# A hybrid decoder trunk on one NeuronCore: a gate block moved ahead of the first window scores, dense weights requested one pair earlier, merge splits written one product later

## The chip, the cores and the metric

The kernel runs on one core of a Trainium2 chip. The time is the device time of one execution in microseconds (us). Three runs of the kernel before gave 2102.69, 2104.17 and 2104.78 us; the median, 2104.17 us, is the time before.

## The reference

Two layers of a decoder trunk work on a sequence of 1024 positions with 1024 channels, in float32. Each layer normalises its input and multiplies it by one wide matrix, whose columns feed three token mixers and their gates:

```python
h = rms_norm(x, g_pre)
p = h @ w_in
(u_a, v_a, gate_a, q_b, k_b, v_b, gate_b,
 q_c, k_c, v_c, gate_c, merge_logits) = jnp.split(p, offsets, axis=-1)
y_a = chunk_gmlp(u_a, v_a, ...) * silu(gate_a)
y_b = sliding_window_attention(rope(q_b), rope(k_b), v_b, sinks) * silu(gate_b)
y_c = stick_breaking_attention(q_c, k_c, v_c) * silu(gate_c)
gates = sigmoid(merge_logits + b_merge)
merged = gates[0]*(y_a @ w_branch_a) + gates[1]*(y_b @ w_branch_b) + gates[2]*(y_c @ w_branch_c)
x = x + rms_norm(merged @ w_out, g_post)
```

Branch B has 8 query heads of 64 channels, rotary positions on queries and keys, a window of 128 positions and a learned sink per head. The merge logits are 3 x 1024 columns, more than a third of the columns of `w_in`.

## The kernel before

Every float32 operand is kept as two parts, a rounded high part and the rest. `split` (L104-112) makes them: ACT casts the high part (L111) and DVE subtracts it from the operand (L112). Every product is then three matmuls on PE, `mm3` (L126-130): high by high (L128), high by low (L129), low by high (L130). All work arrays of 1024 columns come from 27 slots of SBUF, handed out by `new()` and given back by `done()` in first-in, first-out order. Raw weights land in tiles `wr` (two buffers), their split parts live in a tag `w` with six buffers, and there are two PSUM buffers for each of three tags (`pj`; `z` with the tile `pz`; `ta` with the tiles `ptr` and `pav`).

The order of PE's instructions is the order in which the program writes them. The other engines, and SP, which issues the DMAs, get their order from the framework's scheduler, which goes by priorities and by when it reckons that an instruction can start; what it chose is fixed in the program, and each engine works its list off from the front.

A layer runs through these stages:

- A stream of projection jobs (`stream`, filled by `queue_layer`). One job projects 128 columns of `w_in` for all positions: 48 matmuls of 128x512. `raw` makes the jobs of branch B's raw queries, `gate` those of the gate paths. ACT empties the PSUM tile of a query job (L275), then `after_q` applies `rope`: four DMAs swap halves of the channels (L288, on SP), POOL multiplies by sine and cosine (L289, L290), DVE adds (L291), and ACT and DVE split the result into two tiles by heads (L342, L343). `need(x)` runs the stream on PE up to and including job x; `fill(n)` runs n units of it, a job being 10 to 11 units.
- Branch C, with jobs of the stream between its own steps.
- Branch B (`branch_b`): `scores(v)` for v = 0 to 7, two for each pair of heads `hp`; each is 16 matmuls (L486), then copies by ACT and DVE (L492-499), the row maximum (L503), 8 exponentials (L507) with the sum on ACT, and a product by the reciprocal on DVE (L511). `transp` turns the result through PE (L519), `split` makes its parts and POOL masks them (L526); `attend` multiplies by the values (L543). Between these, `fill(FB[..])` gives PE jobs of the stream. The start is `need(("qb", 0))`, `fill(5)`, `scores(0)`, `fill(FB[0])` with `FB[0]` = 10, `scores(1)`.
- The dense stage (`dense`): 13 pairs of column blocks of 256 (a last gate block and the merge logits), each done by Strassen's way in 7 products of 12 matmuls. `prep(p)` loads a pair's weights in two DMAs (L733-737), makes the seven operands (POOL at L748, L750, L751 and L758, `split` for each), one at a time through a generator that `prod` keeps five operands ahead. DVE combines the products (L795). For a merge block ACT applies the sigmoid with the bias (L818) and SP stores the result to DRAM as `sg` (L819). Gate tasks (L708-713: SP's loads and stores, DVE, ACT) are done along the way.
- The merges (`merges`): branches c, b, a in this order, 8 row blocks each, in two halves; per half 12 matmuls, a multiplication by the loaded gate on DVE (L909), an addition (L912; on POOL, on DVE for the last two row blocks of branch a), and for branch a a split of the sum (L111, L112).
- The output projection (`project_out`), which reads these parts, the residual and the norms.

Of the kernel before, what the change touches and what calls it, by code (L numbers as in the profile page):

```python
# [22 lines left out]
P = 128  # L23
T = 1024
D = 1024
KD = D // P
# [7 lines left out]
O_M = 4864  # L34
NSLOT = 27
FC = (1.2, 1.2, 1.9, 1.2)
FB = (10, 1.9, 1.9, 2.2, 2.8, 2.8)
FB_MORE = {1: 2.3, 2: 1.3}


# [1 line left out]
def trunk(ctx, tc, x, w_in, gm_w_s, gm_b_s, gm_g, sinks, w_ba, w_bb, w_bc, b_merge, w_out,  # L42
# [198 lines left out]
    def queue_layer(l, S):  # L241
# [116 lines left out]
        gate("b", 3)  # L358
        for hp in range(4):
            raw(("qb", hp), O_QB + hp * P, 0.125, lambda hp=hp: after_q(hp))  # L360
            if hp < 2:
                gate("a", hp)

        def ua(c):
            def ev(hf, acc):
# [105 lines left out]
    def branch_b(l, S):  # L471
# [86 lines left out]
                nc.sync.dma_start(S["ob"][hp * P:(hp + 1) * P, :], o)  # L558
                done(o)

        need(("qb", 0))
        fill(5)
        ready = {0: scores(0)}
        fill(FB[0])
# [151 lines left out]
    def dense(l, S):  # L716

        T = S["T"].T
        pairs = [(O_GA + 2 * P, "g", ("a", 2))]
        pairs += [(O_M + "abc".index(br) * D + dm * P, "m", (i, br, dm)) for i, br in enumerate("cba")  # L720
                  for dm in range(0, KD, 2)]

        def rhs(nm, k):
            if nm in T:
                hi, lo = T[nm][k // 2]
                return [t.rearrange("p (k t) -> p k t", k=2)[:, k % 2] for t in (hi, lo)]
            hf, kh = {"B11": (0, 0), "B21": (0, 1), "T3": (1, 0), "B22": (1, 1)}[nm]
            return h[hf][0][:, kh * 4 + k], h[hf][1][:, kh * 4 + k]

        def prep(p):  # L730

            col = pairs[p][0]
            raw = []  # L733
            for q in range(2):
                t = wp.tile([P, 4, 256], F32, name="wr", tag="wr", bufs=2)
                nc.sync.dma_start(t, w_in[l, q * 512:(q + 1) * 512, col:col + 256].rearrange("(k p) c -> p k c", p=P))
                raw.append(t)
            a11, a21, a12, a22 = (raw[q][:, :, r * P:(r + 1) * P] for q in range(2) for r in range(2))

            def op(r):  # L740
                w = wp.tile([P, 2, 4, P], F32R, name="wop", tag="w", bufs=6)
                split(w[:, 0], w[:, 1], r)
                return w
            yield op(a11)
            yield op(a12)
            t3 = new()
            s3 = t3[:, :512].rearrange("p (k c) -> p k c", k=4)
            nc.gpsimd.tensor_tensor(s3, a11, a21, op=ALU.subtract)  # L748

            nc.gpsimd.tensor_tensor(a21, a21, a22, op=ALU.add)  # L750
            nc.gpsimd.tensor_tensor(a11, a21, a11, op=ALU.subtract)  # L751
            yield op(a11)
            w = op(s3)
            done(t3)
            yield w
            yield op(a21)
            yield op(a22)
            nc.gpsimd.tensor_tensor(a12, a12, a11, op=ALU.subtract)  # L758
            yield op(a12)

        ops = []
        preps = [prep(p) for p in range(len(pairs))]

        def left(n):
            while len(ops) <= min(n, 7 * len(pairs) - 1):
                ops.append(next(preps[len(ops) // 7]))

        def prod(n, nm):
            left(n + 5)
            w, acc = ops[n], bank()  # L770
            for k in range(4):
                mm3(acc, (w[:, 0, k], w[:, 1, k]), rhs(nm, k), k == 0, k == 3)
            return acc

        left(3)
        S["T"].go(0)
        while step() is not None:
            pass
        S["T"].go(0)
        assert S["T"].left is None  # L780
        S["T"].place_t3()
        a = branch_a(l, S)
        next(a)
        tasks = deque([lambda br=br, c=c: gate_task(S, br, c) for br in "cba" for c in range(4)])
        then = {0: lambda: next(a), 1: lambda: (next(a), next(a)), 2: lambda: (next(a), next(a))}
        for p, (col, kind, what) in enumerate(pairs):
            n = 7 * p
            u = new()
            out = [new(), new()]
            u2, u3 = u[:, :512], u[:, 512:]  # L790
            c11, c12, c21, c22 = (t[:, j * 512:(j + 1) * 512] for t in out for j in range(2))

            def add(o, x, b):
                with tc.high_priority():
                    nc.vector.tensor_tensor(o, x, b, op=ALU.add)  # L795
            p1 = prod(n, "B11")
            if p == len(pairs) - 1:
                S["first"] = load_y(S, "c", True)
            with tc.high_priority():
                nc.scalar.copy(c12, p1)  # L800
            add(c11, c12, prod(n + 1, "B21"))
            add(u2, c12, prod(n + 2, "T2"))
            if p in then:
                then[p]()
            add(u3, u2, prod(n + 3, "T3"))
            p5 = prod(n + 4, "T1")
            add(c22, u3, p5)
            add(u2, u2, p5)
            add(c21, u3, prod(n + 5, "T4"))
            add(c12, u2, prod(n + 6, "B22"))  # L810
            done(u)
            for j in range(2):
                if kind == "g":
                    br, c = what
                    nc.sync.dma_start(S["g" + br][(c + j) * P:(c + j + 1) * P, :], out[j])
                else:
                    i, br, dm = what
                    nc.scalar.activation(out[j], out[j], AF.Sigmoid, bias=bmv(l, "abc".index(br), dm + j))  # L818
                    nc.sync.dma_start(S["sg"][(i * KD + dm + j) * P:(i * KD + dm + j + 1) * P, :], out[j])  # L819
            done(*out)  # L820
            if p >= 1 and tasks:
                tasks.popleft()()
                if p % 2 and tasks:
                    tasks.popleft()()
        assert not tasks
        for t in T.values():
            for q in t:
                done(*q)
# [34 lines left out]
    def merges(l, S):  # L863
# [4 lines left out]
        order = ["c", "b", "a"]  # L868
        blocks = [(bi, br, dm) for bi, br in enumerate(order) for dm in range(KD)]
        wl, sgs = {}, {}  # L870

        def load(i):
            if i < len(blocks) and i not in wl:
# [14 lines left out]
        for i, (bi, br, dm) in enumerate(blocks):  # L888
# [11 lines left out]
            for hf in range(2):  # L900
# [4 lines left out]
                with tc.high_priority():  # L905
                    if bi == 0:
                        nc.vector.tensor_tensor(acc[dm][:, ts], sg[:, ts], z, op=ALU.mult)
                    else:
                        nc.vector.tensor_tensor(sg[:, ts], sg[:, ts], z, op=ALU.mult)  # L909
                if bi:  # L910
                    eng = nc.vector if bi == 2 and dm > KD - 3 else nc.gpsimd
                    eng.tensor_tensor(acc[dm][:, ts], acc[dm][:, ts], sg[:, ts], op=ALU.add)  # L912
                if bi == 2:
                    split(hi[:, ts], lo[:, ts], acc[dm][:, ts])
            done(sg)
            if bi == 2:
                done(acc[dm])
                mg.append((hi, lo))
            if bi == 0 and dm < 4:
                ys.setdefault("b", []).extend(load_y(S, "b", c=dm))  # L920
# [5 lines left out]
                load_wo(l, 0, dm * 2)  # L926
            if bi == 1 and dm == KD - 1:
                done(*S["yslots"])
        return mg

    xs = [x] + [dr.tile([T, D], F32, name=f"xs{l}") for l in range(1, L)] + [out]
# [174 lines left out]
```

## Time and profile before

| | |
|---|---|
| median of 3 runs | 2104.17 us (2102.69 to 2104.78) |
| profiled execution, its time | 2100.85 us |
| its span, first to last instruction | 2099.1 us |
| PE busy | 2034.7 us, 97% |
| DVE busy | 1171.5 us, 56% |
| ACT busy | 780.6 us, 37% |
| POOL busy | 497.9 us, 24% |
| mean granted TensorE clock | 0.990 |
| DMA moved | 245.03 MB, mean 117 GB/s |

The times of the trace count from the start of the span, so 1.75 us of the profiled execution's 2100.85 us lie around it. Busy PE is not PE at its peak: at the half level of the clock a matmul takes longer and still counts as busy. Layer 1 repeats layer 0 some 1040 us later.

### The profile page before, as it was taken

The page shows a single profiled execution, that of the slowest core. Times are in us where ns is not written, and L with a number is a line of the kernel's source. Part 1 is how long each engine was busy: PE and PEld are TensorE (multiplying, and loading weights), DVE is VectorE, ACT ScalarE, POOL GpSimd, SP SyncE. Part 2 cuts the span into 40 slices and gives each one's busy share as a digit, 9 for nine tenths or more (in the row PEclk, how much of TensorE's full clock was granted, in tenths as well). Part 3 has the DMA queues.
Part 4 walks back from the last instruction along what each step waited for, and adds up shares of the span by engine and source line. Part 5 has one row for each costly group of instructions (what it writes and reads, how often), then busy time and mean ns, then how long its engine had stood idle before and what let it go on. Part 6 is the DMA issues. An engine that isn't in the chain of part 4 may idle for free. (4 is left out here: it accounts for less than half of the span.)

```text
span 2099.1 us, 26470 instructions
## 1 busy us (share of the span) xinstructions
PE 2034.7 (97%) x10289; PEld 1700.7 (81%) x10289; DVE 1171.5 (56%) x1521; ACT 780.6 (37%) x1437; POOL 497.9 (24%) x485
## 2 busy tenths in 40 slices
PE   8999998999999999999999999989999999999998
PEld 7898886799887788887898988867988877888876
DVE  5455543468667766544545555344786676565433
ACT  5334333445324334212334334244553343432121
POOL 0121211133542331240002112112344333202400
PEclk9999999999999999999999999999999999999999
DMA  4112122112168538633321111312112775466213
GB/s 161 41 51 67 55 91 70 61 51 71 40 223 285 175 132 290 229 101 91 109 72 50 42 61 60 102 60 71 61 46 76 255 256 171 159 252 220 81 51 130
DMA packets 156253, 245.03 MB, mean 117 GB/s; under 512 B 8104, under 2 KB 113632, under 8 KB 156128
## 3 DMA queue, kind: packets, MB, share of 16 engines
q1 hardware_dynamic: 156128, 243.34, 34.6%
q8 instruction: 81, 1.33, 0.3%
q14 instruction: 44, 0.36, 0.1%
HBM read 166.76 MB, written 71.30 MB: 113 GB/s over the span
## 5 line engine op out<-in xcount | busy, mean ns | idle before, releaser
L128 PE MATMUL pj<-h,whi 128*128 128x512 f32 x968 | 392.4, 405 | 0.0
L129 PE MATMUL pj<-h,whi 128*128 128x512 f32 x968 | 383.5, 396 | 0.0
L130 PE MATMUL pj<-h,wlo 128*128 128x512 f32 x968 | 382.8, 395 | 0.0
L130 PEld LDWEIGHTS pj<-h,wlo 128*128 128x128 f32 x968 | 182.3, 188 | 43.7
L128 PEld LDWEIGHTS pj<-h,whi 128*128 128x128 f32 x968 | 183.2, 189 | 36.0
L129 PEld LDWEIGHTS pj<-h,whi 128*128 128x128 f32 x968 | 183.0, 189 | 34.3
L112 DVE TENSOR_TENSOR wop<-wr,wop 128x512 fp32r<-128x512 f32 x156 | 144.2, 929 | 109.3 <-ACT wop L111 105.9
L112 DVE TENSOR_TENSOR wlo<-wr,whi 128x1024 fp32r<-128x1024 f32 x96 | 128.8, 1342 | 93.6 <-ACT whi L111 93.2
L111 ACT CAST whi<-wr 128x1024 fp32r<-128x1024 f32 x96 | 100.5, 1049 | 185.9 <-PE pj L129 99.4
L111 ACT CAST wop<-wr 128x512 fp32r<-128x512 f32 x156 | 96.1, 617 | 183.8 <-DMA wr<-in_w_in_dram 102.1
L128 PE MATMUL pj<-whi,h 128*128 128x256 f32 x512 | 146.9, 287 | 0.0
L130 PE MATMUL pj<-whi,h 128*128 128x256 f32 x512 | 143.7, 281 | 0.6 <-DVE h L112 0.6
L398 DVE TENSOR_TENSOR_SCAN s<-s,ones 128x128 f32<-128x128 f32 (+3 forms) x64 | 88.4, 1382 | 99.1 <-POOL s L393 98.9
L129 PE MATMUL pj<-wlo,h 128*128 128x256 f32 x512 | 143.5, 280 | 0.0
L112 DVE TENSOR_TENSOR s<-ptr,s 128x512 fp32r<-128x512 f32 (+2 forms) x132 | 77.6, 592 | 106.6 <-ACT s L111 106.1
L912 POOL TENSOR_TENSOR s<-s,s 128x512 f32<-128x512 f32 x56 | 77.5, 1387 | 235.2 <-DVE s L909 130.2
L111 ACT CAST s<-ptr 128x512 fp32r<-128x512 f32 (+2 forms) x132 | 66.8, 506 | 118.8 <-PE ptr L415 110.3
L128 PE MATMUL pj<-h,s 128*128 128x512 f32 x256 | 102.6, 401 | 4.9 <-ACT s L111 3.5
L393 POOL TENSOR_SCALAR_AFFINE_SELECT s<-s 128x128 f32<-128x128 f32 x64 | 23.3, 364 | 346.1 <-ACT s L392 339.7
L111 ACT CAST s<-s 128x512 fp32r<-128x512 f32 (+2 forms) x64 | 47.9, 751 | 150.8 <-POOL s L912 69.7
L130 PE MATMUL pj<-h,s 128*128 128x512 f32 x256 | 101.8, 398 | 1.8 <-DVE s L112 1.8
L129 PE MATMUL pj<-h,s 128*128 128x512 f32 x256 | 101.5, 396 | 0.0
(227 smaller groups left out, 4700.6 us busy)
## 6 DMA issues: line engine op xcount, KB each, us to landing
wr<-in_w_in_dram SPq DMA_DIRECT2D x124, 512.0 KB, 4.1
sg<-s SPq DMA_DIRECT2D x48, 512.0 KB, 5.0
s<-sg SPq DMA_DIRECT2D x48, 512.0 KB, 5.1
s<-in_x_dram SPq DMA_DIRECT2D x16, 512.0 KB, 4.3
wor<-in_w_out_dram SPq DMA_DIRECT2D x16, 512.0 KB, 3.7
s<-s SPq DMA_DIRECT2D x40, 128.0 KB, 2.3
gc<-s SPq DMA_DIRECT2D x8, 512.0 KB, 2.7
oc<-s SPq DMA_DIRECT2D x8, 512.0 KB, 2.8
```

Of the source, the lines that this page charges most:

```text
L111: nc.scalar.copy(hi, raw)
L112: nc.vector.tensor_tensor(lo, raw, hi.bitcast(F32), op=ALU.subtract)
L128: nc.tensor.matmul(acc, lh, rh, start=first, stop=False)
L129: nc.tensor.matmul(acc, lh, rl, start=False, stop=False)
L130: nc.tensor.matmul(acc, ll, rh, start=False, stop=last)
L393: nc.gpsimd.affine_select(t1[:, dg], t1[:, dg], pattern=[[-1, P]], compare_op=ALU.is_gt, fill=1.0, base=0, channel_multiplier=1)
L398: nc.vector.tensor_tensor_scan(t1[:, :kl][:, ::-1], t1[:, :kl][:, ::-1], ones.to_broadcast([P, kl]), 1.0, op0=ALU.mult, op1=ALU.mult)
L912: eng.tensor_tensor(acc[dm][:, ts], acc[dm][:, ts], sg[:, ts], op=ALU.add)
```

## The change

Three things are done, for both layers.

First, the gate block `ga1` is queued behind `qb2` instead of behind `qb1`, branch B starts with `need("ga0")` instead of `need(("qb", 0))`, and `FB[0]` is 4 instead of 10. Secondly, a pair's weights are asked for by a new function `begin`, called for pair p + 1 at the head of pair p; odd pairs above 2 get two of the 27 slots in place of the two `wr` buffers, and the stores of `sg` are issued by ACT instead of SP. Thirdly, in the last branch of the merges the split of a half is put into a list and called behind the multiplication of the next half.

```diff
-FB = (10, 1.9, 1.9, 2.2, 2.8, 2.8)
+FB = (4, 1.9, 1.9, 2.2, 2.8, 2.8)
...
             raw(("qb", hp), O_QB + hp * P, 0.125, lambda hp=hp: after_q(hp))
-            if hp < 2:
-                gate("a", hp)
+            if hp in (0, 2):
+                gate("a", hp // 2)
...
-        need(("qb", 0))
+        need("ga0")
         fill(5)
...
-            col = pairs[p][0]
-            raw = []
-            for q in range(2):
-                t = wp.tile([P, 4, 256], F32, name="wr", tag="wr", bufs=2)
-                nc.sync.dma_start(t, w_in[l, q * 512:(q + 1) * 512, col:col + 256].rearrange("(k p) c -> p k c", p=P))
-                raw.append(t)
+            begin(p)
+            raw, slots = raws.pop(p)
...
             nc.gpsimd.tensor_tensor(a12, a12, a11, op=ALU.subtract)
-            yield op(a12)
-
+            w = op(a12)
+            done(*slots)
+            yield w
...
+        def begin(p):
+
+            if p < len(pairs) and p not in begun:
+                begun.add(p)
+                raws[p] = ([], [])
+                for q in range(2):
+                    if p % 2 and p > 2:
+                        t = new()
+                        raws[p][1].append(t)
+                        t = t.rearrange("p (k c) -> p k c", k=4)
+                    else:
+                        t = wp.tile([P, 4, 256], F32, name="wr", tag="wr", bufs=2)
+                    col = pairs[p][0]
+                    nc.sync.dma_start(t, w_in[l, q * 512:(q + 1) * 512, col:col + 256]
+                                      .rearrange("(k p) c -> p k c", p=P))
+                    raws[p][0].append(t)
...
             n = 7 * p
+            begin(p + 1)
             u = new()
...
-                    nc.sync.dma_start(S["sg"][(i * KD + dm + j) * P:(i * KD + dm + j + 1) * P, :], out[j])
+                    nc.scalar.dma_start(S["sg"][(i * KD + dm + j) * P:(i * KD + dm + j + 1) * P, :], out[j])
...
+                if late:
+                    late.pop()()
                 if bi:
                     eng = nc.vector if bi == 2 and dm > KD - 3 else nc.gpsimd
                     eng.tensor_tensor(acc[dm][:, ts], acc[dm][:, ts], sg[:, ts], op=ALU.add)
                 if bi == 2:
-                    split(hi[:, ts], lo[:, ts], acc[dm][:, ts])
+                    def parts(hi=hi, lo=lo, a=acc[dm], hf=hf, ts=ts):
+                        split(hi[:, ts], lo[:, ts], a[:, ts])
+                        if hf:
+                            done(a)
+                    late.append(parts)
...
+        late.pop()()
         return mg
```

On PE the change moves whole matmuls and changes none. Between the last matmul of `qb0` and the first of `scores(0)` there were 24 matmuls of 128x512 (the first half of `ga0`), and there are now 72 (`ga0` and the first half of `qb1`). Between `scores(0)` and `scores(1)` there were 48 and are now 21; behind `scores(1)` come 18 as before, then the first transposes (L519), and the rest of the sequence up to `scores(2)` has the same counts.

ACT's list from the first scores of layer 0 on, before (L275 with `s24_3234` is the emptying of `qb1`'s first half):

```order
L492 COPY s23_3135<-pz_3136 128x2x128
L493 COPY s23_3135<-pz_3136 128x2x128
L498 COPY s23_3135<-pz_3151 128x512
L507 ACT_TABLE_LOAD
L507 ACTIVATE s23_3135,ls_3163<-s23_3135,mx_3162 128x128 x8
L508 ACTIVATE es_3164<-es_3164 128x8
L111 CAST whi_3331<-wr_3329 128x1024
L275 ACTIVATE s24_3234<-pj_3209 128x512
```

And the same place now (L275 with `s23_3189` empties `qb1`, first half from `pj_3164`, second half from `pj_3191`):

```order
L275 ACTIVATE s23_3189<-pj_3164 128x512
L492 COPY s24_3195<-pz_3196 128x2x128
L493 COPY s24_3195<-pz_3196 128x2x128
L498 COPY s24_3195<-pz_3211 128x512
L507 ACT_TABLE_LOAD
L507 ACTIVATE s24_3195,ls_3223<-s24_3195,mx_3222 128x128 x2
L275 ACTIVATE s23_3189<-pj_3191 128x512
L507 ACTIVATE s24_3195,ls_3223<-s24_3195,mx_3222 128x128 x6
L508 ACTIVATE es_3224<-es_3224 128x8
```

The first half of `qb1` is now emptied ahead of the first softmax, and the emptying of its second half stands between the second and the third of the 8 exponentials.

POOL's list at the same place, before (L494 masks the first scores, L526 the transposed ones, L289 and L290 are the rotary products of `qb1`):

```order
L494 AFFINE_SELECT s23_3135<-s23_3135 128x2x128
L526 AFFINE_SELECT s12_3306<-s6_3305 128x512 x2
L526 AFFINE_SELECT s13_3351<-s19_3350 128x512 x2
L289 TENSOR_TENSOR s9_3315<-s9_3315,s17_2857 128x1024
L290 TENSOR_TENSOR s24_3234<-s24_3234,s15_2856 128x1024
```

And now:

```order
L494 AFFINE_SELECT s24_3195<-s24_3195 128x2x128
L526 AFFINE_SELECT s22_3349<-s21_3348 128x512 x2
L289 TENSOR_TENSOR s4_3262<-s4_3262,s17_2857 128x1024
L290 TENSOR_TENSOR s23_3189<-s23_3189,s15_2856 128x1024
L526 AFFINE_SELECT s18_3375<-s13_3374 128x512 x2
```

The rotary products moved ahead of the second pair of masks, and still stand behind the first pair.

DVE's list at the end of the last branch of layer 0, before (L909 multiplies a half, L912 adds it, L112 with slots is the split of that half, L112 with `wor` that of an output weight):

```order
L909 TENSOR_TENSOR s19_7680<-s19_7680,pj_7758 128x512
L912 TENSOR_TENSOR s9_7138<-s9_7138,s19_7680 128x512
L112 TENSOR_TENSOR s18_7757<-s9_7138,s16_7756 128x512
L909 TENSOR_TENSOR s19_7680<-s19_7680,ptr_7775 128x512
L912 TENSOR_TENSOR s9_7138<-s9_7138,s19_7680 128x512
L112 TENSOR_TENSOR s18_7757<-s9_7138,s16_7756 128x512
L909 TENSOR_TENSOR s22_7718<-s22_7718,pz_7794 128x512
L912 TENSOR_TENSOR s20_7175<-s20_7175,s22_7718 128x512
L112 TENSOR_TENSOR h11_75<-wor_7832,h10_74 128x1024
```

And now, where the same two lines are numbered L928 and L933:

```order
L928 TENSOR_TENSOR s12_7678<-s12_7678,pj_7756 128x512
L933 TENSOR_TENSOR s10_7138<-s10_7138,s12_7678 128x512
L112 TENSOR_TENSOR s3_7755<-s10_7138,s21_7754 128x512
L928 TENSOR_TENSOR s12_7678<-s12_7678,ptr_7773 128x512
L933 TENSOR_TENSOR s10_7138<-s10_7138,s12_7678 128x512
L112 TENSOR_TENSOR s3_7755<-s10_7138,s21_7754 128x512
L928 TENSOR_TENSOR s11_7716<-s11_7716,pz_7792 128x512
L933 TENSOR_TENSOR s26_7175<-s26_7175,s11_7716 128x512
L112 TENSOR_TENSOR h11_75<-wor_7832,h10_74 128x1024
```

Slots differ; the sequence of lines doesn't.

## Rows read from the trace of the kernel before

**Rows 1.** The page's first part: busy time of each engine, its share of the span, and the count of its instructions.

```profile
PE 2034.7 (97%) x10289; PEld 1700.7 (81%) x10289; DVE 1171.5 (56%) x1521; ACT 780.6 (37%) x1437; POOL 497.9 (24%) x485
```

**Rows 2.** The view of waits, for PE: what PE stood still for, us in total, times, longest.

```profile
PE pz L486 <- DVE s L343: 25.1, 8, 7.8
...
PE pz L130 <- DVE wop L112: 5.3, 5, 1.9
...
PE pj L128 <- ACT s L111: 3.5, 2, 1.7
...
PE pj L130 <- DVE s L112: 1.8, 2, 0.9
...
PE pj L128 <- DVE s L909: 1.4, 2, 0.7
PE pz L128 <- ACT wop L111: 1.3, 2, 1.2
```

**Rows 3.** The view by stretches, for four stretches around the first and the third scores of each layer and one in the dense stage of layer 1: length, busy time (and count) of PE, PEld, DVE, ACT and POOL, the granted clock, the DMA share, GB/s.

```profile
360.30:370.50 10.20, 6.32 (x22) 5.54 (x23) 5.33 (x6) 3.32 (x5) 0.41 (x1) 0.50 0.00 0
401.30:408.10 6.80, 5.64 (x20) 4.98 (x21) 3.04 (x5) 1.70 (x4) 0.41 (x1) 0.50 0.00 0
1401.40:1408.20 6.80, 4.06 (x17) 3.76 (x18) 2.88 (x3) 2.67 (x4) 0.41 (x1) 0.50 0.00 0
1438.90:1445.70 6.80, 4.34 (x17) 3.99 (x18) 2.88 (x3) 2.54 (x5) 0.41 (x1) 0.50 0.00 0
1749.50:1752.90 3.40, 3.40 (x10) 2.65 (x9) 3.40 (x6) 1.29 (x3) 0.97 (x1) 0.50 0.01 5
```

**Rows 4.** The timeline of PE around the first and the third scores of layer 0: start, duration, what, and in brackets PE's idle time before it.

```profile
355.54 0.40 PE L130 MATMUL pj<-h,wlo 128*128 128x512 f32 x1
...
363.72 0.80 PE L486 MATMUL pz<-s,s 128*128 128x256 f32 x2 [7.79 <-DVE s L343]
...
364.98 3.36 PE L486 MATMUL pz<-s,s 128*128 128x256 f32 x14 [0.46 <-DVE s L343]
...
402.00 0.80 PE L486 MATMUL pz<-s,s 128*128 128x256 f32 x2 [3.92 <-DVE s L343]
```

**Rows 5.** The timeline of ACT, SP, POOL and DVE ahead of the first scores of layer 0: the way of `qb0` from its last matmul to the operands of `scores(0)`.

```profile
350.39 0.59 ACT L275 ACTIVATE s<-pj 128x512 f32<-128x512 f32 x1
...
351.00 2.43 SPq L288 DMA_DIRECT2D s<-s  x4
...
355.44 2.35 POOL L289 TENSOR_TENSOR s<-s,s 128x1024 f32<-128x1024 f32 x1 [29.68 <-DMA s<-s]
...
360.11 1.23 DVE L291 TENSOR_TENSOR s<-s,s 128x1024 f32<-128x1024 f32 x1 [8.38 <-POOL s L290]
361.37 2.11 ACT L342 CAST s<-s 64x1024 fp32r<-64x1024 f32 x2 [5.52 <-DVE s L291]
362.45 2.47 DVE L343 TENSOR_TENSOR s<-s,s 64x1024 fp32r<-64x1024 f32 x2 [1.11 <-ACT s L342]
```

**Rows 6.** The timeline of ACT, DVE and POOL behind the first scores of layer 0: one exponential, the emptying of a gate block by DVE, the last step of the softmax, a copy of the second scores, two masks on POOL, and the low part of a stream weight.

```profile
372.61 0.40 ACT L507 ACTIVATE s<-s,mx 128x128 f32<-128x128 f32 x1
...
374.33 0.69 DVE L249 COPY s<-pj 128x512 f32<-128x512 f32 x1 [2.89 <-PE pj L130]
...
376.38 1.22 DVE L511 TENSOR_TENSOR s<-s,ls 128x1024 f32<-128x1024 f32 x1
...
382.20 0.73 DVE L499 COPY_PREDICATED s<-mprev,pz 128x512 f32<-128x512 int32 x1 [3.46 <-ACT s L498]
...
387.97 1.36 POOL L526 TENSOR_SCALAR_AFFINE_SELECT s<-s 128x512 fp32r<-128x512 f32 x2 [20.45 <-ACT s L111]
...
391.86 1.22 DVE L112 TENSOR_TENSOR wlo<-wr,whi 128x1024 fp32r<-128x1024 f32 x1
```

**Rows 7.** The view by stretches, PE alone, for the part of each layer's dense stage that holds all its waits for weights, and for a part that holds none: length, PE busy (and its count of matmuls, here all 128x512), granted clock, DMA share, GB/s.

```profile
645.00:715.00 70.00, 66.56 (x277) 1.00 0.64 222
1680.00:1756.00 76.00, 71.45 (x291) 0.98 0.66 228
800.00:870.00 70.00, 70.00 (x302) 1.00 0.67 236
```

**Rows 8.** The costliest groups of ACT between 620 and 905 us, the dense stage of layer 0 (us busy, mean ns of one, idle time before them by releaser).

```profile
L111 ACT CAST wop<-wr 128x512 fp32r<-128x512 f32 x58 | 35.7, 616 | 63.3 <-DMA wr<-in_w_in_dram 33.1 <-POOL wr L751 21.7 <-PE ptr L130 3.3
L818 ACT ACTIVATE s<-s,vec 128x1024 f32<-128x1024 f32 x22 | 25.3, 1149 | 20.8 <-DVE s L795 20.8
L711 ACT ACTIVATE s<-s 128x1024 f32<-128x1024 f32 x10 | 10.6, 1062 | 23.0 <-DVE s L710 19.3 <-DMA wr<-in_w_in_dram 3.6
```

**Rows 9.** The page's DMA issues, two of them: count, KB each, median us from issue to landing.

```profile
wr<-in_w_in_dram SPq DMA_DIRECT2D x124, 512.0 KB, 4.1
sg<-s SPq DMA_DIRECT2D x48, 512.0 KB, 5.0
```

**Rows 10.** The view by stretches, PE alone, for the end of the merges of both layers, all matmuls 128x512; columns as in rows 7.

```profile
958.00:973.00 15.00, 11.67 (x43) 0.89 0.22 67
1997.00:2012.00 15.00, 11.66 (x48) 1.00 0.18 60
```

**Rows 11.** The timeline of DVE for two successive multiplications in the last branch of layer 0, on the way to that end.

```profile
955.74 0.68 DVE L909 TENSOR_TENSOR s<-s,pz 128x512 f32<-128x512 f32 x1
...
959.14 0.68 DVE L909 TENSOR_TENSOR s<-s,pj 128x512 f32<-128x512 f32 x1
```

More of the change, by code (lines that the diff above doesn't have):

```diff
@@ L758, in prep @@
             nc.gpsimd.tensor_tensor(a12, a12, a11, op=ALU.subtract)
-            yield op(a12)
+            w = op(a12)
+            done(*slots)
+            yield w
+        raws = {}
+        def begin(p):
[13 more added lines that the diff above has]
+                    raws[p][0].append(t)
+        begun = set()
         ops = []
@@ L870, in merges @@
         wl, sgs = {}, {}
+        late = []
         def load(i):
@@ L913, in merges @@
                 if bi == 2:
-                    split(hi[:, ts], lo[:, ts], acc[dm][:, ts])
+                    def parts(hi=hi, lo=lo, a=acc[dm], hf=hf, ts=ts):
[3 more added lines that the diff above has]
+                    late.append(parts)
             done(sg)
             if bi == 2:
-                done(acc[dm])
                 mg.append((hi, lo))
```

## The prediction

> **What bounds the kernel now.** I read the page's busy times first: PE is busy for 2034.7 us of 2099.1 [rows 1], so a change that leaves every matmul in place can win only PE's standing time (64.4 us) and what a slow clock adds. The waits of PE name the places [rows 2]: scores waiting for the low part of the rotated queries (L343) 25.1 us in 8 waits; dense products waiting for a weight operand, 5.3 us by DVE and 1.3 by ACT; products waiting at the end of the merges, 3.5, 1.8 and 1.4. The view by stretches adds the clock: 0.50, the 1.2 GHz level, at the first and third scores of both layers and once in the dense stage [rows 3]. The timeline shows the largest wait: PE ends the cover at 355.54, idles 7.79 us, runs two matmuls, idles 0.46; the third scores wait 3.92 us [rows 4].
>
> Priced with the clock: PE was busy for 6.32 + 5.64 + 4.06 + 4.34 = 20.4 us in those four half-clock stretches [rows 3], of which half, 10.2, is loss. Part one of the change thus aims at 25.1 + 10.2 = 35.3 us. For the dense stage I compare with an undisturbed stretch of 302 matmuls in 70 us, 0.232 us each [rows 7]: 277 in 70 us are 25 too few, 5.8 us; 291 in 76 us where 328 would fit are 37 too few, 8.6 us. Part two aims at 14.4 us (the 3.4 us at half clock are in it). By the same measure the end of the merges loses (64.7 - 43) x 0.232 = 5.0 and (64.7 - 48) x 0.232 = 3.9 us [rows 10], 8.9 for part three.
>
> **Part one, the first scores.** The way of `qb0` starts at 350.39 with its emptying; four DMAs, two POOL products (2.35 each), the add on DVE at 360.11, then ACT and DVE; the first L343 is done when PE starts at 363.72, the second at 364.98 [rows 4, 5]. Before, 24 matmuls covered it, so `qb0` ended on PE at about 355.77 - 24 x 0.232 = 350.2. Now 72 stand there, 16.7 us, and PE arrives at 366.9. DVE has a new errand in between: it empties the second half of `ga0` (L249, 0.69 us [rows 6]) ahead of L291, and can't before PE ends `ga0` at 350.2 + 11.1 = 361.3. So L291 starts at about 362.2 instead of 360.11, and the two L343 end at 365.8 and 367.1. PE wants the second after two matmuls, at 367.2. Both waits go, with at most 0.1 us left, and the clock should not fall.
>
> What is late next? Call S the start of `scores(0)`. The 16 matmuls took 0.80 + 3.36 = 4.2 us at half clock, so about 2.0 at full. Then come 21 matmuls (4.9), `scores(1)` (2.0), 18 matmuls (4.2): PE wants the first softmax at S + 13.1. But ACT's list now has the emptying of `qb1`'s second half between the second and third exponential, and this waits for three matmuls behind `scores(1)`: PE ends them at S + 2.0 + 4.9 + 2.0 + 0.7 = 9.6. Add 0.6 for the emptying, as in [rows 5], six exponentials of 0.40 (2.4), the small steps on the sums (0.6: eight exponentials from 372.61 end at 375.8, L511 starts at 376.38) and L511 (1.22) [rows 6]: S + 14.4. A new wait of about 1.3 us at the first transposes. Bounds: 0, if the modelled ends of matmuls flatter PE, and 2.5, if ACT first does other queued work.
>
> Third scores: POOL's products for `qb1` stand behind the first masks. After that wait the first transposes end at S + 14.9; ACT's cast takes them to 15.5, but DVE has L511, two L499 (0.73 each) and a low part of a stream weight (1.22) queued ahead of the split (0.7, the size of L249), ending at about S + 17.8 [rows 6]. The mask behind it takes 0.68, L289 and L290 4.7: S + 23.2. From the start of L291 to the two L343 were 3.6 and 4.9 us [rows 5]: S + 26.8 and 28.1. PE wants them at 13.1 + 1.3 + 8 transposes and 6 L543 (an L486 at full clock, 0.12, at most for each, 1.5) + 42 matmuls (9.7) = S + 25.7, and the second after two matmuls. So this wait shrinks from 3.92 + 0.46 to about 1.1 + 1.1. Bounds 0.5 and 4.
>
> Together 3.5 us per layer remain. The clock may fall in such a cluster: in the dense stage of layer 1 it fell behind waits of no more than 1.9 us [rows 2, 3]. Half-clock stretches at the scores cost 2.0 to 3.2 us, one of 3.4 us costs 1.7 [rows 3]; I take half of that, 0.9. The Trainium skill (TensorE: Matmul & The Clock Gate, Why this matters for your kernels) blames long idle gaps between matmul bursts; by it short waits cost only themselves and 0.9 would go. The row at 1749.5 speaks against leaving it at that. Part one keeps 4.4 us per layer, 8.8 in all, and wins 35.3 - 8.8 = 26.5 us, with bounds of 18 (9 us kept per layer) and 35.3 (nothing kept). `qb2` comes earlier than before and `qb3` no later, so the fifth and seventh scores, which don't wait now, should not start to.
>
> **Part two, weights a pair early.** ACT's casts of weight operands stood idle for 33.1 us waiting for the DMA and 21.7 for POOL's combination (L751) [rows 8]. A pair's load (4.1 us to land [rows 9]) could start only when the previous pair's last operands had freed both `wr` tiles, then casts, DVE subtractions and POOL steps followed in series. With the loads a pair ahead, and from the third odd pair on in slots, the series starts 20 us earlier (7 products x 12 x 0.232 = 19.5 us a pair), against waits of at most 1.9 us. What is late next are POOL's combinations, on an engine that is busy for 24% of the span [rows 1], and the ring of six `w` buffers, neither near its limit. The first three pairs still share `wr`, where some short waits may stay. I take 12 of the 14.4; bounds 0 and 14.4.
>
> The 48 stores leave SP for ACT. SP wins free queue time that PE doesn't wait for. ACT issues 24 per layer, two per pair; at SP's 2.43 us for four [rows 5] that is 1.2 us per pair. Its dense work per pair is some 9 us of 19.5: seven casts of 0.616, two sigmoids of 1.149, one to two gate tasks of 1.062 [rows 8] and a copy of a half, like the 0.59 in [rows 5]. Cost nothing while no store waits long at the head of ACT's list. If that cover is gone, rival four applies.
>
> **Part three, the splits.** The sequence of lines on DVE at the end of the last branch is the same before and after, as on ACT and POOL. The chain of one half there, multiply, add, cast, subtract, paced the multiplications at 959.14 - 955.74 = 3.40 us [rows 11] against 12 x 0.232 = 2.78 for a product. With the same list it paces them still: no gain, no loss. Bounds 0 and the 8.9 us.
>
> **Sum.** 2100.85 - 26.5 - 12 - 0 = 2062.4 us for a profiled execution. The median of the runs lies 3.3 us above the profiled one: 2065.7, and I say 2065.
>
> **The rivals.**
> One: both rotary waits go wholly and all dense waits too: 2100.85 - 35.3 - 14.4 + 3.3 = 2054. For it: the waits that I derive at the transposes and third scores hang on differences of 1 us between sums of twenty terms. Against: the new place of the emptying in ACT's list is fixed.
> Two: the early weights win nothing, since the stores hold up casts on ACT by about what the early loads win, or the transfers themselves are slow beside the rest (DMA share 0.64 there [rows 7]): 2100.85 - 26.5 + 3.3 = 2078. A store must wait for its sigmoid and for the DMA that used its completion counter before. The Trainium skill (DMA: Bandwidth & Descriptors, Issuing engines are not separate DMA queues) says that ACT's DMAs run on the same 16 engines and only issue time is saved; by it the moved stores can't speed the loads, and what is won comes from asking early alone. Against this rival: undisturbed PE at a like DMA share of 0.67 in the third stretch.
> Three: the splits also take effect: 2065.7 - 8.9 = 2057. Against it speaks the unchanged list.
> Four, slower: ACT becomes the bound of the dense stage. A pair has 19.5 - 9 - 1.2 = 9.3 us of ACT to spare, 4.6 per store. A store that stood at the head for a full landing, 5.0 us [rows 9], and 1.6 more behind other transfers would overrun each pair by 4 us, and 24 such pairs cost 96 us, 2065.7 + 96 = 2162. It outweighs the gains of 38.5 us from 1.6 us per pair on, at 5.4 us a store. Against it: a store's counter was last used eight DMAs ago, by transfers mostly landed.
>
> **How the numbers follow.** My forecast 0.50, rival one 0.20, two 0.20, three 0.04, four 0.04, something I don't see 0.02, split evenly. The range runs from 2050, rival one less the 3 to 4 us that runs differ by, to 2086, where part one wins its lower bound and part two nothing (2100.85 - 18 + 3.3). It leaves out rival four and the far ends, somewhat under 2 in 10. A measurement can tell 0.2%, some 4.2 us, from no change: faster needs less than 2100, which all cases but the fourth and half of the unseen give; for small mishaps I leave 0.03 within 0.2%. Faster 0.93, same 0.03, slower 0.04.
>
> **What would show it.** In PE's waits, L486 falls from 25.1 us to about 4 to 5, the 7.8 is gone, and a new row of about 2.6 us appears for L519 waiting for L511. The granted clock stays at full at the first scores. Waits for `wop` nearly vanish and the two dense stretches hold about 300 and 325 matmuls. The 3.5, 1.8 and 1.4 at the end of the merges stay. A long wait of ACT for a DMA at the stores, or L486 waits above 9 us a layer, would prove the forecast wrong.

## The result and the profile after

The changed kernel takes 2080.18 us (median of 4 runs, 2079.33 to 2083.93) against 2103.43 us for the kernel before (4 runs, 2101.91 to 2104.78): a ratio of 0.9889, 95% interval 0.9871 to 0.9908. It is 23.3 us faster, where 38.5 were forecast; the time lies in the forecast's range of 2050 to 2086, near its upper end and near rival two's 2078. The profiled execution took 2083.93 us with a span of 2082.2 us, so it is the slowest of the four, and the traces differ by 16.9 us of span only.

In the new code more lines have moved: L813 is the dense combinations (L795 before), L818 is now the copy of a pair's first product on ACT (L800), L836 the sigmoid (L818), L837 the store of `sg` on ACT.

The view of waits of the changed kernel, for PE (us in total, times, longest), to be held against [rows 2]:

```profile
PE ptr L519 <- DVE s L554: 12.1, 6, 2.8
PE ptr L633 <- ACT s L818: 10.4, 2, 6.7
...
PE pj L128 <- ACT s L111: 3.5, 2, 1.7
PE pj L129 <- DVE s L112: 2.4, 2, 1.8
...
PE pj L130 <- DVE s L112: 1.8, 2, 0.9
PE pz L486 <- DVE s L343: 1.5, 2, 0.7
PE pj L128 <- DVE s L928: 1.5, 2, 0.7
```

The 25.1 us at the scores (L486) became 1.5, and every wait for a `wop` operand is gone. Two others took their place. The second row, L633, was not there before; the first was smaller, in the same view of the kernel before:

```profile
PE ptr L519 <- DVE s L554: 3.5, 4, 0.9
```

The three rows of the end of the merges read 3.5, 1.8 and 1.5, against 3.5, 1.8 and 1.4 before.

The view by stretches of the changed kernel, all engines (columns as in [rows 3]), at the first scores of layer 0, at the third scores, and at two new places:

```profile
367.30:374.30 7.00, 7.00 (x39) 6.02 (x38) 2.73 (x5) 3.25 (x8) 0.41 (x1) 1.00 0.04 13
391.90:396.00 4.10, 3.30 (x22) 2.87 (x22) 3.68 (x8) 3.61 (x8) 0.67 (x1) 1.00 0.46 106
...
606.20:610.40 4.20, 4.20 (x14) 3.72 (x15) 3.01 (x5) 2.02 (x4) 2.51 (x2) 0.50 0.42 173
532.00:535.40 3.40, 3.40 (x10) 2.63 (x9) 2.75 (x4) 2.13 (x6) 1.21 (x1) 0.50 0.45 130
```

At the scores the clock is at its full level. Behind the first scores of layer 0 ACT empties the second half of `qb1` (L275) between the exponentials, and PE turns the first softmax (L519), both without idle time in brackets:

```profile
374.65 0.58 ACT L275 ACTIVATE s<-pj 128x512 f32<-128x512 f32 x1
```

```profile
380.41 0.60 PE L519 MATMUL ptr<-ident,s 128*128 128x128 f32 x4
```

Half clock now stands at 606, behind the new wait of L633, and at 532, in the last part of branch B. Layer 1 has it at the same two places: at 1636 behind L633, and twice around the end of branch B, at 1552.6 and 1583.4, for about 3.3 us each.

The same view for PE alone in the dense stage of both layers (columns as in [rows 7]):

```profile
640.00:710.00 70.00, 70.00 (x302) 1.00 0.71 251
1665.00:1741.00 76.00, 76.00 (x328) 1.00 0.72 255
```

302 and 328 matmuls are what undisturbed PE does in 70 and 76 us; before there were 277 and 291. So both aims were reached nearly in full, and rather more than half of what they won was lost at the two new places. Their working:

The first is at pair 2 of the dense stage. The timeline of ACT and of PE there, changed kernel, layer 0:

```profile
596.32 1.06 ACT L711 ACTIVATE s<-s 128x1024 f32<-128x1024 f32 x1 [5.22 <-DVE s L710]
597.29 2.17 ACT L836 ACTIVATE s<-s,vec 128x1024 f32<-128x1024 f32 x2
598.45 1.37 ACTq L837 DMA_DIRECT2D sg<-s  x2
600.43 1.06 ACT L711 ACTIVATE s<-s 128x1024 f32<-128x1024 f32 x1 [0.97 <-DVE s L710]
605.56 0.59 ACT L818 COPY s<-ptr 128x512 f32<-128x512 f32 x1 [4.07 <-DMA sg<-s]
```

```profile
606.20 2.08 PE L633 MATMUL ptr<-s,s 128*128 128x128 f32 x8 [6.75 <-ACT s L818]
```

The copy that empties PSUM for pair 2's first product stands still for 4.07 us until a store of `sg` has read its source. The list of ACT tells why: the copy writes the slot of `s18_5101`, which pair 1 has just handed back.

```order
L836 ACTIVATE s18_5101<-s18_5101,vec_80 128x1024
L836 ACTIVATE s19_5100<-s19_5100,vec_80 128x1024
L837 DMA sg0_93<-s18_5101 128x1024
L837 DMA sg0_93<-s19_5100 128x1024
L711 ACTIVATE s20_5272<-s20_5272 128x1024
L818 COPY s18_5284<-ptr_5289 128x512
```

Two slots more are held by pair 3's early weights, so the queue of free slots is short enough there for a slot to come back while its store is in flight. PE's matmuls of branch A (L633) need the PSUM buffer, and the half clock follows. Not all of PE's wait is the store's: PE stood from 599.45 on, while the second sigmoid of the gate tasks, which stands ahead of the copy in ACT's list, ended only at 601.49. By this reading 4.07 of the 6.75 us are the store's. In layer 1 the copy waits 4.05 us for its store and PE 3.65.

The second place is the end of branch B. ACT's timeline of the changed kernel, layer 0:

```profile
493.92 1.28 ACT L615 ACT_TABLE_LOAD   x1
...
500.01 1.28 ACT L507 ACT_TABLE_LOAD   x1
```

The same load in the kernel before, behind the last softmax, whose last exponential (L508) started at 515.25:

```profile
516.42 1.28 ACT L615 ACT_TABLE_LOAD   x1
```

And PE in the changed kernel:

```profile
500.73 0.63 PE L519 MATMUL ptr<-ident,s 128*128 128x128 f32 x4 [1.78 <-DVE s L554]
520.19 0.63 PE L519 MATMUL ptr<-ident,s 128*128 128x128 f32 x4 [2.76 <-DVE s L554]
529.48 0.39 PE L543 MATMUL pav<-s,s 128*128 128x256 f32 x1 [0.48 <-POOL s L526]
531.05 0.86 PE L543 MATMUL pav<-s,s 128*128 128x256 f32 x5 [1.18 <-POOL s L526]
```

The square root of branch A's normalisation (L615) now falls between the last two softmaxes, with a table load for it and another for the exponentials behind it. Normalisation on DVE and pair 0's POOL steps moved up with it, and the emptying of `attend`'s PSUM (L553, L554), for which the transposes wait, came late behind them.

### The profile page after: what moved, and what is told of

It is laid out like the page before. It is cut to its first block, busy times and chain, and to the rows that moved or that the text cites. A ratio compares the mean times of both kernels' runs of the same rounds, so it can differ in the third digit from the quotient of the medians.

```text
span 2082.2 us, 26420 instructions
## 1 busy us (share of the span) xinstructions
PE 2029.6 (97%) x10289; PEld 1701.0 (82%) x10289; DVE 1179.6 (57%) x1521; ACT 786.2 (38%) x1439; POOL 500.7 (24%) x485
## 4 chain that ended last, share of the span: by engine, by line
PE 82%; DVE 6%; POOL 4%; DMA 3%; ACT 3%; issue 3%; SPq 0%; DVEq 0%; POOLq 0%; ACTq 0%
PE pj L128 17%; PE pj L130 17%; PE pj L129 17%; PE pz L129 5%; PE pz L128 5%; PE pz L130 5%; PE ptr L129 4%; PE ptr L128 4%; PE ptr L130 4%; DMA wr<-in_w_in_dram 2%; PE ptr L415 2%; POOL s L678 1%; PE pz L486 1%; PE pav L130 1%; PE pav L129 1%
## 5 line engine op out<-in xcount | busy, mean ns | idle before, releaser
L129 PE MATMUL pj<-h,whi 128*128 128x512 f32 x968 | 384.2, 397 | 0.0
L129 PEld LDWEIGHTS pj<-h,whi 128*128 128x128 f32 x968 | 182.8, 189 | 34.4
L112 DVE TENSOR_TENSOR wlo<-wr,whi 128x1024 fp32r<-128x1024 f32 x96 | 125.6, 1308 | 87.9 <-ACT whi L111 87.8
L111 ACT CAST whi<-wr 128x1024 fp32r<-128x1024 f32 x96 | 100.8, 1050 | 168.9 <-PE pj L129 101.6
L129 PE MATMUL pj<-wlo,h 128*128 128x256 f32 x512 | 143.7, 281 | 0.0
L933 POOL TENSOR_TENSOR s<-s,s 128x512 f32<-128x512 f32 x56 | 77.7, 1390 | 240.0 <-DVE s L928 208.4
L112 DVE TENSOR_TENSOR s<-ptr,s 128x512 fp32r<-128x512 f32 (+2 forms) x132 | 77.7, 591 | 101.0 <-ACT s L111 100.4
L111 ACT CAST s<-s 128x512 fp32r<-128x512 f32 (+2 forms) x64 | 47.9, 752 | 171.1 <-POOL s L933 69.8
L111 ACT CAST s<-ptr 128x512 fp32r<-128x512 f32 (+2 forms) x132 | 66.8, 506 | 119.7 <-PE ptr L415 110.3
L112 DVE TENSOR_TENSOR wop<-wr,wop 128x512 fp32r<-128x512 f32 x96 | 87.6, 918 | 33.9 <-ACT wop L111 33.7
L129 PE MATMUL pj<-h,s 128*128 128x512 f32 x256 | 102.0, 399 | 0.0
L130 PEld LDWEIGHTS pj<-whi,h 128*128 128x128 f32 x512 | 96.9, 189 | 1.2 <-DVE h L112 1.2
```

What stands on the lines that cost most here:

```text
L111: nc.scalar.copy(hi, raw)
L112: nc.vector.tensor_tensor(lo, raw, hi.bitcast(F32), op=ALU.subtract)
L129: nc.tensor.matmul(acc, lh, rl, start=False, stop=False)
L130: nc.tensor.matmul(acc, ll, rh, start=False, stop=last)
```

## The experiments

Each of the ten is compared with runs of the kernel before on the same chip, whose medians were 2102.0 us (the first four), 2105.05 us (the next four) and 2103.67 us (the last two). Where medians of two batches are subtracted below, the ratios give the same differences within 4 us.

**Which part costs what.** Part one alone, and parts two and three alone. The edits are those of the change's diff, for the first:

```diff
-FB = (10, 1.9, 1.9, 2.2, 2.8, 2.8)
+FB = (4, 1.9, 1.9, 2.2, 2.8, 2.8)
...
-            if hp < 2:
-                gate("a", hp)
+            if hp in (0, 2):
+                gate("a", hp // 2)
...
-        need(("qb", 0))
+        need("ga0")
```

and for the second these lines are as before, with all others as in the changed kernel.

> Part one alone on the kernel before (ga0 ahead of the first scores, ga1 behind qb2, FB[0] 4). Theory A: the new order of the stream wins about 33 us at the first and third scores and itself costs about 15 us at the end of branch B (transposes and attends late, 6.8 us in layer 0 and 8.2 in layer 1), so some 18 us are left: about 2085 us, a ratio near 0.991, with the waits of L519 and L543 at the end of branch B as in the changed kernel, and the dense waits for weights (some 14 us) as before. Rival B: the loss at the end of branch B comes from part two, whose early pair 0 and 1 loads put POOL and ACT work ahead of the masks; then part one alone wins all 33: about 2070 us, and the L519 waits stay near 3.5 us.

Measured: 2083.51 us, ratio 0.9906 (0.9889 to 0.9923). The waits of PE:

```profile
PE ptr L519 <- DVE s L554: 12.0, 6, 2.7
...
PE pz L130 <- DVE wop L112: 6.1, 6, 2.4
...
PE pz L486 <- DVE s L343: 1.5, 2, 0.8
```

Theory A: the loss at the end of branch B comes with part one, without any early weights, and the dense waits stay. Part one alone wins 18.5 us.

> Parts two and three alone (the order of branch B as before). Theory A: waits for weight operands vanish (14 us), but the copy of pair 2's first product (L818) waits for the store of the slot that it writes, so L633 waits some 10 us with the half clock behind it, about 13.6 us lost: near 2103 us, ratio 0.998 to 1.002. Rival B: that wait arises only with the changed order of branch B (other slots in the queue); then about 14 us are won: 2089 us, ratio 0.993. Rival C: the loss at the end of branch B belongs to part two: slower, some 2115 us.

Measured: 2097.17 us, ratio 0.9973 (0.9963 to 0.9982). The waits of PE:

```profile
PE pz L486 <- DVE s L343: 25.3, 8, 7.8
...
PE ptr L633 <- ACT s L818: 5.1, 2, 3.1
PE ptr L519 <- DVE s L554: 3.5, 4, 0.9
...
PE pz L130 <- DVE wop L112: 1.3, 1, 1.3
```

The kind of loss is theory A's, its size half: 5.1 us at L633. Rivals B and C fall: the wait at L633 arises with the old order of branch B too, and L519 stays at 3.5 us. Parts two and three win 4.8 us alone, not 14. How long the copy waits hangs on when a store lands, and differs from trace to trace: L633 has 10.4 us in the changed kernel's, 10.6 in e4's, 5.6 in e5's and 4.1 in e8's.

**Is it the slot?** In the first of two, pair p's own arrays are taken from the queue before the next pair's weights; in the second, SP issues the stores again.

```diff
-            begin(p + 1)
             u = new()
             out = [new(), new()]
+            begin(p + 1)
```

> The changed kernel with begin(p + 1) behind the three new() calls of pair p, so that the output arrays get the slots that have been free longest and the early weights those just stored from. Theory A (a slot taken while its store is in flight): the wait of L633 for ACT (10.4 us) goes, and with its half clock about 13 us: near 2067 us, ratio to before 0.983. Rival B (ACT is held up by the stores at the head of its list or by the gate tasks, whatever the slots): no change, 2080 us, and L633 still waits.

Measured: 2091.42 us, ratio 0.9946 (0.9931 to 0.9961). Theory A's forecast of the time fell, and rival B's too. L633 doesn't wait any more, but others do:

```profile
PE pz L128 <- ACT wop L111: 10.0, 2, 5.2
...
PE pz L128 <- DVE s L636: 4.5, 2, 2.7
```

Pair 3's early weights now got the slots with stores in flight. The timelines of POOL, SP and ACT show where that went: POOL stood for 22.19 us until they had landed, with a product of branch A (L639) behind; SP's list held the store of that product (L640) until 617.33, with the gate tasks' loads behind; and ACT held a gate task's sigmoid until 631.94, with casts of weights behind.

```profile
608.91 1.27 POOL L744 TENSOR_TENSOR s<-s 128x512 f32<-128x512 f32 x1 [22.19 <-DMA s<-in_w_in_dram]
```

```profile
617.33 5.52 SPq L640 DMA_DIRECT2D oa<-s  x2
```

```profile
631.94 1.06 ACT L711 ACTIVATE s<-s 128x1024 f32<-128x1024 f32 x1 [10.50 <-DVE s L710]
```

So it isn't enough to hand the slots out in another order: there are too few of them at this point, and whoever gets the last ones waits.

```diff
-                    nc.scalar.dma_start(S["sg"][(i * KD + dm + j) * P:(i * KD + dm + j + 1) * P, :], out[j])
+                    nc.sync.dma_start(S["sg"][(i * KD + dm + j) * P:(i * KD + dm + j + 1) * P, :], out[j])
```

> The changed kernel with the stores of sg issued by SP again. Theory A (slot reuse): the copy L818 still waits for the landing of the store, so the L633 wait stays at 10 us or more and the time at 2080 us, or 0 to 5 us slower. Rival B (a store at the head of ACT's list holds up ACT): the L633 wait goes, about 2067 us.

Measured: 2080.87 us, ratio 0.9900 (0.9881 to 0.9919), and the wait is there:

```profile
PE ptr L633 <- ACT s L818: 10.6, 2, 5.5
```

The engine that issues the stores decides nothing here that these runs could tell (0.7 us between the medians, 2.3 by the ratios); theory A.

**The two losses taken away.** First the stream at the end of branch B:

```diff
-FB_MORE = {1: 2.3, 2: 1.3}
+FB_MORE = {}
```

> The changed kernel without the extra fills behind the first transposes of v = 1 and 2 (FB_MORE empty), so that the stream of jobs stands at the end of branch B about where it stood before (the change had run it 21 matmuls ahead, this takes some 17 back). Theory A (the stream runs ahead, so that the square root's table load, the normalisation and pair 0's POOL work fall among the last softmaxes): the L519 waits fall from 12 us to about 4, some 15 us of loss at the end of branch B go, and 2 to 4 us of new waits appear at v = 1 and 2: near 2068 us. Rival B (the loss comes from the order of the jobs, qb2 ahead of ga1): the end of branch B stays as it is, 2080 us or slower by the new waits.

Measured: 2065.18 us, ratio 0.9802 (0.9774 to 0.9830), 15.0 us below the changed kernel's median. The waits of PE:

```profile
PE ptr L633 <- ACT s L818: 5.6, 2, 3.8
PE ptr L519 <- DVE s L554: 5.1, 6, 1.9
```

Theory A. The square root's table load stands behind the last exponential again (499.25 us, L508 at 498.08). The new waits expected at v = 1 and 2 didn't come: L519 has 1.5 us there, as in the changed kernel. Since L633 waited 4.8 us less in this trace than in the changed kernel's, the 15.0 us are checked below by a pair of runs in which it doesn't wait at all. Which of the things that came with the position of the stream (table loads, normalisation, pair 0's steps) cost how much, this doesn't tell.

Then the slots, by leaving out the gate tasks of pair 1; the later pairs do them:

```diff
-            if p >= 1 and tasks:
+            if p >= 2 and tasks:
```

> The changed kernel with the gate tasks starting at pair 2 instead of pair 1, so that the four slots which they took at pair 1 are left for pair 2's outputs and pair 3's weights. Theory A (too few slots, one taken while its store is in flight): the L633 wait (10.4 us) and the half clock behind it go without a new wait of a weight operand, 13 us won: about 2067 us. Rival B (wherever the slots run short, some consumer waits): L633 or wop waits of 8 us or more remain, 2078 us or more.

Measured: 2068.28 us, ratio 0.9824 (0.9798 to 0.9850). Neither L633 nor any `wop` appears among PE's waits; the other loss stays:

```profile
PE ptr L519 <- DVE s L554: 12.0, 6, 2.7
```

Theory A by the time. But this edit frees four slots and takes two sigmoids of gate tasks out of ACT's list at the same point. In the changed kernel's trace 4.07 us of ACT's idling ended with the store, and 0.97 and 5.22 just before with DVE's step of a gate task; the runs don't separate the two. The reading of the trace above gives the store the larger share.

> Both edits together. If both theories A hold the gains add, since the places are 50 us apart: about 2055 us. If only one does, 2067 us; if neither, 2080 us.

Measured: 2052.08 us, ratio 0.9747 (0.9721 to 0.9772). The gains add: 15.0 and 11.9 us alone, 28.1 together. Against e6, where L633 doesn't wait either, moving the stream wins 16.2 us; against e5, the freed slots win 13.1. What is left of PE's waits is the start, the end of the merges and small ones:

```profile
PE ptr L519 <- DVE s L554: 4.6, 5, 1.9
PE pj L128 <- ACT s L111: 3.4, 2, 1.7
PE pj L130 <- DVE s L112: 1.8, 2, 0.9
PE pj L128 <- DVE s L928: 1.5, 2, 0.7
```

**Part three.** The changed kernel with the split written in its old place:

```diff
-                if late:
-                    late.pop()()
...
-                    late.append(parts)
+                    split(hi[:, ts], lo[:, ts], acc[dm][:, ts])
```

> The changed kernel with the splits of branch a written where they were before (part three undone). Theory A (the scheduler's order on DVE, ACT and POOL there is the same either way): 2080 us, within 0.2%, and the same waits at the end of the merges. Rival B: part three hides something that the order of lines does not show: 4 us slower or more.

Measured: 2080.14 us, ratio 0.9882 (0.9851 to 0.9912), 0.04 us from the changed kernel's median and 1.5 by the ratios, nothing clear of the spread. Theory A; the waits at the end of the merges are the same (3.4, 1.8 and 1.4). Since e8 ran beside e5, e6 and e7, their gains of 15.0, 11.9 and 28.1 us hold within one batch too. What could be had there was tried in another way, on top of e7:

```diff
-                    eng = nc.vector if bi == 2 and dm > KD - 3 else nc.gpsimd
+                    eng = nc.vector if bi == 2 and dm > 1 else nc.gpsimd
```

> The kernel of e7 (both edits) with the additions of the last branch (L933) on DVE from row block 2 on, where POOL did them up to block 5. Theory A (the chain multiply, add, cast, subtract paces the halves at 3.40 us against 2.78 for a product, since a POOL addition takes 1.28 us and a DVE one 0.69): the pace of L928 falls to 2.7 to 2.8 us, the waits of project_out for these parts (3.4, 1.8 and 1.5 us) shrink to under 3 in all, and with the clock some 6 us are won: near 2046 us, ratio near 0.972. Rival B (these waits belong to the output weights' parts queued on DVE between the last halves, not to the pace): 2052 us, the same waits.

Measured: 2043.57 us, ratio 0.9723 (0.9703 to 0.9743), 8.5 us below e7's median (5 by the ratios, whose intervals overlap; the slowest of e9's four runs is 6.2 us below the fastest of e7's), the fastest of all. The waits for L111, L112 and L928 at the end of the merges have left PE's list, and the timeline of DVE shows the pace, 2.70 us between multiplications:

```profile
923.49 0.68 DVE L928 TENSOR_TENSOR s<-s,ptr 128x512 f32<-128x512 f32 x1
...
926.19 0.68 DVE L928 TENSOR_TENSOR s<-s,pz 128x512 f32<-128x512 f32 x1
...
928.89 0.68 DVE L928 TENSOR_TENSOR s<-s,pj 128x512 f32<-128x512 f32 x1
```

Last, e7 with the stores on SP, the same edit as in e4:

> The kernel of e7 with the stores of sg issued by SP. Theory A (which engine issues them decides nothing, as at e4): 2052 us, within 3. Rival B (with the slots no longer short, ACT's stores are what keep the loads early): 2058 us or more, with waits for wop back.

Measured: 2053.72 us, ratio 0.9768 (0.9742 to 0.9793), 1.6 us from e7's median, within the expected 3, but 4.4 by the ratios, whose intervals overlap. No wait for `wop` came back. Theory A, as far as these runs can tell: with slots enough, too, the early loads win, whichever engine issues the stores.

## Why the prediction was right, and where it wasn't

The direction was right, and the time in its range. The size was not: 23.3 us instead of 38.5. That the range holds is partly luck: its upper end stood for waits that stay at the scores (18 us won by part one) and nothing from part two. Part one alone did win only 18.5 us [e1], but the scores gave up nearly all their waits, and the loss came at a place that the sum doesn't have.

- Part one at the scores: forecast 26.5 us won of 35.3, since 3.5 us of waits and 0.9 for the clock per layer were to stay. L486 kept 1.5 us in both layers together and the clock stayed at 1.00, so some 33.8 were won there. The term of the sum that was mis-sized is what stays: 4.4 us a layer forecast, about 0.75 measured. The first pair of waits went as derived: PE ran straight into `scores(0)` at 367.5. The step that failed is the emptying of `qb1` between the second and the third exponential. The prediction puts its last three matmuls behind `scores(1)`; they stand ahead of it, and those behind it belong to the next job. The slip comes from the count of PE's order: between `qb0` and `scores(0)` stand 27 matmuls before and 75 now, not 24 and 72, because running a job to its end also starts the next one by three matmuls. So the 21 matmuls between the scores finish `qb1`. In the trace L275 ran at 374.65 without waiting, L511 ended at 379.3 where S + 14.4 would have been 381.9, and the first transposes at 380.41 didn't wait. The third scores came as derived in kind: one wait of about 0.7 us per layer in place of 1.1 + 1.1. The 0.9 for the clock rested on that cluster and fell with it.
- The end of branch B: this is the step that cost most. I asked whether later scores would wait for their queries, found that they wouldn't, and priced nothing else there. But 21 more matmuls of the stream ahead of `scores(1)` bring everything that hangs on the stream forward, up to branch A's statistics, among the last softmaxes. The term stood at nothing in the sum. L519's waits rose by 8.6 us, L129 got a row of 2.4, and three half-clock stretches of 3.3 to 3.4 us cost some 1.7 more each: about 16 us. e1 puts the loss with part one; moving the stream alone gave back 15.0 us [e5 against the changed kernel] and 16.2 [e7 against e6].
- Part two: forecast 12 of 14.4 us; the waits for operands went whole. The step that failed is the one on what is late next: POOL and the six `w` buffers were named, the 27 slots weren't, although the diff takes two of them for odd pairs. The loss is 11.9 us by e6 and 13.1 by e7 against e5. It is neither rival two (the stores hold casts up on ACT) nor rival four (ACT as the bound of the whole stage): it comes once per layer and with either issuing engine [e4]. Rival four's place, a list that stands still until a store has landed, was near it, but by way of the slot and not of the store's own turn. The prediction's sign of being wrong, a long wait of ACT for a DMA at the stores, came in this form: 4.07 and 4.05 us at the copy.
- The stores' move: forecast nothing, measured nothing clear of the spread (0.7 and 1.6 us between the medians in e4 and e10, 2.3 and 4.4 by the ratios). The Trainium skill (DMA: Bandwidth & Descriptors, Issuing engines are not separate DMA queues) says that DMAs of all issuing engines run on the same DMA engines, and that issuing from several saves issue time only; these two runs agree with it.
- Part three: forecast nothing, by the list; measured nothing clear of the spread, 0.04 us between the medians [e8]. The 8.9 us at which this place was priced are there to be had in good part: e9 won 5 to 8.5 by a shorter chain.
- The sum by these prices is 33.8 + 14.4 - 15.0 - 11.9 = 21.3 us, against 23.3 between the medians. For part one alone they give 33.8 - 15.0 = 18.8, against 18.5 in e1; for the rest 14.4 - 11.9 = 2.5, against 4.8 in e2.

## What to carry to other kernels

Where work is pulled forward in a hand-written order, look at the far end of the stage as well: what hangs on the stream moves up too, and a table load that stood behind the last softmax can land between two. When buffers are taken from a shared queue for earlier loads, ask for each later taker which store or load last held its buffer, and how long ago; a change of order among the takers only moves the wait. And read the list that the scheduler made: written order alone (part three) moved nothing, while a shorter chain did.

## What the runs showed of the hardware

Two of DVE's smallest operations took more than ten times as long beside POOL's rotary products in the changed kernel, and ended when these ended (L504 and L505 on 128x8 take 0.17 us elsewhere, at 372.33 and 372.53 in the same trace):

```profile
383.52 1.94 DVE L504 SCALAR_TENSOR_TENSOR mx<-mx,nsnk 128x8 f32<-128x8 f32 x1
385.50 2.33 DVE L505 TENSOR_TENSOR es<-mx,snk 128x8 f32<-128x8 f32 x1
```

```profile
383.04 2.40 POOL L289 TENSOR_TENSOR s<-s,s 128x1024 f32<-128x1024 f32 x1
385.40 2.40 POOL L290 TENSOR_TENSOR s<-s,s 128x1024 f32<-128x1024 f32 x1
```

Layer 1 repeats it, with 1.95 and 2.33 us. Not every operation of DVE stood still beside these products: the reduction L503, which began before them at 382.28 and overlapped the first, kept its 1.21 us, and in the kernel before two L554, which read PSUM, took 0.42 and 0.43 us beside L289 and L290, as elsewhere. No run here tells what sets the two kinds apart.

Of the clock, in the changed kernel: the granted level stayed at 1.00 behind the single wait of 2.76 us at 520 and went to 0.50 behind the waits of 0.48 and 1.18 us at 529 and 531. In layer 1 it went to 0.50 behind a single wait of 2.75 us at the same place in the program. So a wait's length alone did not decide it in this trace. The view by stretches, PE alone, behind the two single waits:

```profile
520.00:526.00 6.00, 5.81 (x31) 1.00 0.00 0
1552.60:1556.00 3.40, 3.40 (x9) 0.50 0.00 0
```

The second wait:

```profile
1551.23 0.63 PE L519 MATMUL ptr<-ident,s 128*128 128x128 f32 x4 [2.75 <-DVE s L554]
```
